# A chunked scan between dense matmuls: transposes first, a shared PSUM ring, two products on another engine

## The chip, the cores and the metric

The kernel runs on one core of a Trainium2 chip. Five engines work side by side, each with its own queue: TensorE (PE; its weight loads are listed as PEld), VectorE (DVE), ScalarE (ACT), GpSimd (POOL) and SyncE (SP), which here only issues DMAs. The metric is the device time of one execution in microseconds, median of several runs. [...]

## The reference, cut to what matters

One layer on 1024 tokens of width 1024: three token mixers (two attentions and a state space model), merged with sigmoid gates, and a gated MLP. The change lies in the state space model's scan. With x as 16 heads of 64, B and C as 2 groups of 128, dt per token and head, and a the running sum of dt*A in a chunk:

```python
xdt = xf * dtc[..., None]
decay = jnp.where(causal, jnp.exp(jnp.where(causal, seg, 0.0)), 0.0)   # seg = a_i - a_j
cb = jnp.einsum('bcign,bcjgn->bcijg', Cc, Bc)
y_diag = jnp.einsum('bcijg,bcijgh,bcjghp->bcighp', cb, decay, xdt)
states = jnp.einsum('bcjgn,bcjgh,bcjghp->bcghpn', Bc, decay_to_end, xdt)
def step(h, inp):
    st, dec = inp
    return h * dec[..., None, None] + st, h
y_off = jnp.einsum('bcign,bcghpn,bcigh->bcighp', Cc, h_in, jnp.exp(a_cum))
...
y = (y + xh * D[:, None]).reshape(Bsz, S, SSM_INNER)
return rms_norm(y * jax.nn.silu(z), norm_g)
```

## The kernel before

The program is a chain of stages; PE's order inside the stages around the change is written out by hand, while a scheduler sets the order of the other engines' queues from its own model of time. Two kinds of work are merged on PE:

- **The dense work** ("fill"): 36 column blocks of the input projection, that is 1728 matmuls of 128x512 (`mm`, L794; six of them per step of the generator, counted as 1.3 us). A block's weights are loaded (`wr`), split into a high part by ACT (`wh`, L744) and a low part by DVE (`wl`, L745); ACT evicts each half block (L801), and SP stores it to `g_d` (L808). The dense work depends on nothing in attention or scan, so it is put between their pieces, first in attention, then in the scan.
- **The scan** over eight chunks of 128 tokens. In step c of its loop, `ssd_a` prepares chunk c, `ssd_b` computes chunk c-1, `ssd_c` finishes chunk c-2, and `merge` interleaves them with a budget of dense work, `FILL_SSD[c]` in us of the generator's counting; what is not used is carried over. What is left of the dense work after the scan runs before the next stage.

`ssd_a`: `pcb` is C·B of a group of 8 heads (DVE masks it into `cbm`); `pse` are the exponents of four heads, which ACT turns into `E`; DVE multiplies E by cbm, and ACT and DVE split E into `Eh` and `El`. PE transposes the chunk of x (`xs`, loaded by L1062) into `stp`, and ACT copies this to `xT`, in two halves of 8 heads (g = 0, 1). From xT come three products of 128x1024: `xd` = x·dt (DVE, then split into `xdt` by ACT and DVE), `xdd` = x·decay_to_end·dt (GpSimd, L1113) and the start of `y` = x·D (GpSimd, L1115). `bT` is the transpose of B.

`ssd_b`: `py` are the products of E with xdt, which DVE adds to y; `pof` (L1136) is C times the incoming state, which DVE scales into `yo` and adds to y; `pst` (L1146) is B^T·xdd, which DVE adds to the state `hst` (L1152) after it has scaled the old one (L1151). Then y is multiplied by the gate z (L1155, DVE), squared and summed by ACT into `yss` (L1158, with the buffer `yT` as the place of the squares), and scaled by ACT with the inverse root that DVE finds (L1160, L148 to L159).

`ssd_c`: PE transposes y in two halves (L1171), ACT copies them to `yT` (L1172), and SP stores `yT` to `ys_d` (L1174). There is one `yT` buffer and one `xdd` buffer.

PSUM in the scan: two banks for `pcb` and `pse` ("seg"), two for `py`, one for every transpose ("tp"), one for `pof` and `pst` ("st"), two for the dense work. The stage behind the scan multiplies the three mixers' outputs by their weights (`ybr`, L167); it first loads `ar` and splits it into `ah` (ACT) and `al` (DVE).

Of the kernel before, what the change touches and what calls it, by code (L numbers as in the profile page):

```python
# [11 lines left out]
F32 = mybir.dt.float32  # L12
F32R = mybir.dt.float32r
BF16 = mybir.dt.bfloat16
I32 = mybir.dt.int32
AF = mybir.ActivationFunctionType
# [5 lines left out]
P = 128  # L22
# [20 lines left out]
def block_kernel(ctx: ExitStack, tc: tile.TileContext, x, positions, norm_mix_g, w_in, b_gate,  # L43
# [91 lines left out]
    def uid(s):  # L135
        cnt[0] += 1
        return f"{s}_{cnt[0]}"
# [845 lines left out]
        return 0.88 * jp + 0.33 + 0.39  # L983

    FILL_ATT = 1.08
    FILL_SSD = [10.6] * 8 + [12.0, 30.0]
    with ExitStack() as pt__:
        atp = pt__.enter_context(TP("atp", 2))
        psp = pt__.enter_context(TP("psa", 1, space=PSUM))
# [39 lines left out]
    with ExitStack() as ps__:  # L1029
# [37 lines left out]
        def ssd_a(o, c):  # L1067

            if c + 1 < NT:
                seg_rows(c + 1)  # L1070
                load_bc(obj[c + 1], c + 1)
            xT = pool.tile([P, D], F32, name=uid("xT"), tag="xT", bufs=1)
            o.E = []
            for g in range(2):
                hs = slice(8 * g, 8 * g + 8)
                pcb = psp.tile([P, 512], F32, name=uid("pcb"), tag="seg", bufs=2)
                T.matmul(pcb[:, 0:P], o.bc[:, g, :], o.bc[:, 2 + g, :], start=True, stop=True)
                cbm = pool.tile([P, P], F32, name=uid("cbm"), tag="cbm")
                V.tensor_mul(cbm, pcb[:, 0:P], tri)
                yield 0.22  # L1080
                for q in range(2):
                    pse = psp.tile([P, 512], F32, name=uid("pse"), tag="seg", bufs=2)
                    T.matmul(pse, seg_l[c % 2][:, 2 * g + q, :], seg_r[2 * g + q].rearrange("r h i -> r (h i)"),
                             start=True, stop=False)
                    T.matmul(pse, identb, mssd.rearrange("p h i -> p (h i)"), start=False, stop=True)
                    if c + 1 < NT:
                        seg_cols(c + 1, 2 * g + q)
                    E = pool.tile([P, 4, P], F32, name=uid("E"), tag="E")
                    A.activation(E, pse.rearrange("p (h i) -> p h i", h=4), AF.Exp)
                    V.tensor_mul(E, E, cbm.unsqueeze(1).to_broadcast([P, 4, P]))  # L1090
                    Eh, El = (pool.tile([P, 4, P], F32R, name=uid(n), tag=n, bufs=4) for n in ("Eh", "El"))
                    split(Eh, El, E)
                    o.E.append((Eh, El))
                    yield 0.43
                pt = psp.tile([P, 512], F32, name=uid("stp"), tag="tp", bufs=1)
                for j in range(4):
                    T.transpose(pt[:, j * P:j * P + P], o.xs[:, 4 * g + j, :], ident)
                A.activation(xT[:, 512 * g:512 * g + 512], pt, AF.Copy)
                yield 0.44
            if c + 1 < NT:  # L1100
                load_xs(obj[c + 1], c + 1)
            o.bT = pool.tile([P, 2, P], F32, name=uid("bT"), tag="bT")
            pt = psp.tile([P, 256], F32, name=uid("stp"), tag="tp", bufs=1)
            for g in range(2):
                T.transpose(pt[:, g * P:g * P + P], o.bc[:, g, :], ident)
            A.activation(o.bT, pt.rearrange("p (g n) -> p g n", g=2), AF.Copy)
            xv = xT.rearrange("p (h d) -> p h d", d=64)
            o.xdt = pool.tile([P, 16, P], F32R, name=uid("xdt"), tag="xdt")
            xd = pool.tile([P, 16, 64], F32, name=uid("xd"), tag="xd", bufs=1)
            V.tensor_mul(xd, xv, hb(dt, c))  # L1110
            split(o.xdt[:, :, 0:64], o.xdt[:, :, 64:128], xd)
            o.xdd = pool.tile([P, 16, 64], F32, name=uid("xdd"), tag="xdd", bufs=1)
            G.tensor_mul(o.xdd, xv, hb(dend, c))  # L1113
            o.y = pool.tile([P, 16, 64], F32, name=uid("y"), tag="y", bufs=3)
            G.tensor_mul(o.y, xv, Db.unsqueeze(2).to_broadcast([P, 16, 64]))  # L1115
            yield 0.22

        def ssd_b(o, c, prev):

            zt, _ = f_t4.get()  # L1120
            SY.dma_start(zt, z_d[c * P:c * P + P, :])
            for g in range(2):
                hs = slice(8 * g, 8 * g + 8)
                for q in range(2):
                    py = psp.tile([P, 4, P], F32, name=uid("py"), tag="py", bufs=2)
                    for hh in range(4):
                        h, (Eh, El) = 8 * g + 4 * q + hh, o.E[2 * g + q]
                        T.matmul(py[:, hh, :], Eh[:, hh, :], o.xdt[:, h, :], start=True, stop=False)
                        T.matmul(py[:, hh, 0:64], El[:, hh, :], o.xdt[:, h, 0:64], start=False, stop=True)
                    h4 = slice(8 * g + 4 * q, 8 * g + 4 * q + 4)  # L1130
                    V.tensor_add(o.y[:, h4, :], o.y[:, h4, :], py[:, :, 0:64])
                    V.tensor_add(o.y[:, h4, :], o.y[:, h4, :], py[:, :, 64:128])
                    yield 0.8
                if prev is not None:
                    po = psp.tile([P, 512], F32, name=uid("pof"), tag="st")
                    T.matmul(po, o.bc[:, 2 + g, :], prev.hst[:, hs, :], start=True, stop=True)  # L1136
                    tmp = pool.tile([P, 8, 64], F32, name=uid("yo"), tag="yo", bufs=1)
                    V.tensor_mul(tmp, po.rearrange("p (h d) -> p h d", d=64), hb(ea, c, hs))
                    V.tensor_add(o.y[:, hs, :], o.y[:, hs, :], tmp)
                    yield 0.86  # L1140
            if c + 1 < NT:
                o.hst = pool.tile([P, 16, 64], F32, name=uid("hst"), tag="hst")
                for g in range(2):
                    hs = slice(8 * g, 8 * g + 8)
                    ps_ = psp.tile([P, 512], F32, name=uid("pst"), tag="st")
                    T.matmul(ps_, o.bT[:, g, :], o.xdd[:, hs, :], start=True, stop=True)  # L1146
                    psv = ps_.rearrange("p (h d) -> p h d", d=64)
                    if prev is None:
                        V.tensor_copy(o.hst[:, hs, :], psv)
                    else:  # L1150
                        V.tensor_mul(o.hst[:, hs, :], prev.hst[:, hs, :], hb(cdec, c, hs))  # L1151
                        V.tensor_add(o.hst[:, hs, :], o.hst[:, hs, :], psv)  # L1152
                    yield 0.86
            yf = o.y.rearrange("p h d -> p (h d)")
            V.scalar_tensor_tensor(out=yf, in0=yf, scalar=0.5, in1=zt, op0=ALU.mult, op1=ALU.mult)  # L1155
            o.yT = pool.tile([P, 8, P], F32, name=uid("yT"), tag="yT", bufs=1)
            ss = pool.tile([P, 1], F32, name=uid("yss"), tag="yss")
            A.activation(o.yT.rearrange("p j s -> p (j s)"), yf, AF.Square, accum_out=ss)  # L1158
            v = pool.tile([P, 1], F32, name=uid("yv1"), tag="yv1")
            V.tensor_scalar(v, ss, 1.0 / D, EPS, op0=ALU.mult, op1=ALU.add)  # L1160
            r = pool.tile([P, 1], F32, name=uid("yr1"), tag="yr1")
            rsqrt(pool, r, v, 1)
            A.activation(yf, yf, AF.Copy, scale=r)

        def ssd_c(o, c):

            yf = o.y.rearrange("p h d -> p (h d)")
            for g in range(2):
                pt = psp.tile([P, 512], F32, name=uid("stp"), tag="tp", bufs=1)
                for j in range(4):  # L1170
                    T.transpose(pt[:, j * P:j * P + P], yf[:, (4 * g + j) * P:(4 * g + j + 1) * P], ident)  # L1171
                A.activation(o.yT[:, 4 * g:4 * g + 4, :], pt.rearrange("p (j s) -> p j s", j=4), AF.Copy)  # L1172
                yield 0.44
            SY.dma_start(ys_d[:, :, c * P:c * P + P].rearrange("j p s -> p j s"), o.yT)  # L1174

        with tc.manual_schedule(engines={mybir.EngineType.PE}):
# [3 lines left out]
            for q in range(4):  # L1180
                seg_cols(0, q)
            load_xs(obj[0], 0)
            merge([], 6.0)
            for c in range(NT + 2):
                st = []
                if c < NT:
                    st.append((ssd_a(obj[c], c), 3.4))
                if 0 <= c - 2 < NT:
                    st.append((ssd_c(obj[c - 2], c - 2), 0.88, 0.6 if c <= NT else 0.9))
                if 0 <= c - 1 < NT:  # L1190
                    st.append((ssd_b(obj[c - 1], c - 1, obj.get(c - 2)), 6.6, 0.25 if c < NT else 0.1))
                merge(st, FILL_SSD[c])
# [488 lines left out]
```

## Time and profile before

| | us |
|---|---|
| runs, median of 3 | 2163.03 (2156.59 to 2163.8) |
| profiled execution, time | 2163.26 |
| its span, first to last instruction | 2161.5 |
| TensorE clock granted, mean | 0.982 |

The profile is of one execution. Engine shares are shares of the span. A row of a windows table gives the length of a window, then busy time and number of instructions of PE, PEld, DVE, ACT and POOL, the granted clock of PE (1.00 is full), the DMA engines' share and GB/s. A row of waits reads: who waited, for whom, microseconds in total, times, longest. A row of the timeline gives start, duration, engine, line, operation, output<-inputs, and in brackets how long the engine stood idle before it and what ended that. The scan's first matmul starts at 989.2 us, its last at 1223.2.

### The profile page before, as it was taken

How to read it: one execution, taken by the hardware profiler on the slowest of the kernel's cores; microseconds unless marked ns; L12 is line 12 of the kernel's file. 1: busy time of each engine (PE TensorE's matmuls, PEld its weight loads, DVE VectorE, ACT ScalarE, POOL GpSimd, SP SyncE). 2: the span in 40 equal slices, each digit the busy share in tenths (PEclk: the TensorE clock that was granted, in tenths of full speed). 3: DMA queues.
4: the chain of work that ended last, by engine and by line, in shares of the span. 5: the costliest groups of instructions: out<-in, count | busy, mean ns of one | idle time of the engine just before them, and what ended most of it. 6: DMA issues, size and time to landing. Idle time of an engine off the chain costs nothing.

```text
span 2161.5 us, 29107 instructions
## 1 busy us (share of the span) xinstructions
PE 2053.6 (95%) x10239; PEld 1693.8 (78%) x10253; DVE 1406.9 (65%) x2574; ACT 933.7 (43%) x1669; POOL 689.9 (32%) x636
## 2 busy tenths in 40 slices
PE   7999899999999999999999999999889999999999
PEld 6898787778888787787666788888668888887887
DVE  6687477356656566665888446557976777665655
ACT  5554222145555555554445313223444444544432
POOL 2454132212222222220222022002655454441855
PEclk9999999999999999999999999999899999999999
DMA  5167668554343544524343556342122222229765
GB/s 168 33 186 223 228 211 247 196 147 126 100 131 108 125 125 107 128 87 119 92 117 94 169 178 209 116 151 79 39 88 88 78 88 78 87 71 346 250 210 194
DMA packets 276649, 303.61 MB, mean 140 GB/s; under 512 B 19308, under 2 KB 209784, under 8 KB 276504
## 3 DMA queue, kind: packets, MB, share of 16 engines
q1 hardware_dynamic: 276504, 301.76, 45.5%
q8 instruction: 81, 1.33, 0.3%
q14 instruction: 64, 0.52, 0.1%
HBM read 209.03 MB, written 92.67 MB: 140 GB/s over the span
## 4 chain that ended last, share of the span: by engine, by line
PE 76%; DVE 10%; DMA 5%; ACT 3%; issue 3%; POOL 2%; SPq 0%; DVEq 0%; ACTq 0%; POOLq 0%
PE mm L794 15%; PE dn L1628 10%; PE ybr L167 8%; PE ua L1321 5%; PE uc L1321 4%; PE ud L1321 4%; PE wo L1366 4%; PE fx L167 4%; PE s L884 4%; PE tp L952 3%; PE ub L1321 2%; PE cq L167 1%; PE fxv L167 1%; PE q L167 1%; PE kv L167 1%
## 5 line engine op out<-in xcount | busy, mean ns | idle before, releaser
L794 PE MATMUL mm<-hnh,wh 128*128 128x512 f32 x576 | 251.5, 437 | 0.0
L906 POOL TENSOR_SCALAR pm<-pm,rs 128x128 f32<-128x128 f32 (+7 forms) x128 | 109.6, 859 | 407.3 <-DVE rs L905 256.2
L794 PE MATMUL mm<-hnh,wl 128*128 128x512 f32 x576 | 228.1, 396 | 0.0
L794 PE MATMUL mm<-hnl,wh 128*128 128x512 f32 x576 | 227.3, 395 | 0.0
L1628 PE MATMUL dn<-dr,dr 128*128 128x512 f32 x592 | 182.2, 389 | 0.0
L899 ACT ACTIVATE pm<-s,nmx 128x128 f32<-128x128 f32 (+2 forms) x192 | 110.0, 578 | 98.7 <-DVE nmx L896 69.8
L958 DVE TENSOR_TENSOR ptl<-tp,pth 128x512 fp32r<-128x512 f32 (+1 forms) x160 | 100.3, 633 | 69.7 <-ACT pth L957 68.0
L889 DVE TENSOR_REDUCE nmx<-s 128x1 f32<-128x128 f32 (+2 forms) x192 | 105.6, 553 | 58.8 <-PE s L887 47.0
L884 PE MATMUL s<-qk,qk 96*128 96x384 f32 (+5 forms) x480 | 122.3, 359 | 12.7 <-ACT pm L899 11.0
L957 ACT ACTIVATE pth<-tp 128x512 fp32r<-128x512 f32 (+1 forms) x160 | 88.0, 553 | 100.7 <-PE tp L952 100.2
L1628 PEld LDWEIGHTS dn<-dr,dr 128*128 128x128 f32 x592 | 111.1, 188 | 23.1
L794 PEld LDWEIGHTS mm<-hnh,wl 128*128 128x128 f32 x576 | 109.1, 189 | 25.6
L794 PEld LDWEIGHTS mm<-hnl,wh 128*128 128x128 f32 x576 | 110.2, 191 | 17.8 <-issue 3.4
L794 PEld LDWEIGHTS mm<-hnh,wh 128*128 128x128 f32 x576 | 110.7, 192 | 17.1 <-issue 3.3
L1628 PE MATMUL dn<-dr 128*128 128x512 f32 x296 | 115.2, 389 | 0.0
L167 PE MATMUL fx<-w5h,hnh 128*128 128x512 f32 x256 | 101.9, 403 | 7.0 <-ACT w5h L142 7.0
L143 DVE TENSOR_TENSOR dr<-dr,dr 128x1024 fp32r<-128x1024 f32 x52 | 73.0, 1403 | 54.3 <-ACT dr L142 52.4
L142 ACT ACTIVATE wh<-wr 128x1024 fp32r<-128x1024 f32 (+1 forms) x46 | 41.9, 911 | 144.5 <-PE ybr L167 63.5
L884 PEld LDWEIGHTS s<-qk,qk 96*128 96x128 f32 (+1 forms) x480 | 82.2, 194 | 25.6 <-ACT pm L899 15.0
L167 PE MATMUL fx<-w5h,hnl 128*128 128x512 f32 x256 | 101.8, 399 | 0.0
L167 PE MATMUL ybr<-ah,wh 128*128 128x512 f32 x256 | 99.6, 394 | 1.6 <-ACT ah L142 1.6
L167 PE MATMUL fx<-w5l,hnh 128*128 128x512 f32 x256 | 101.1, 396 | 0.0
(457 smaller groups left out, 5819.1 us busy)
## 6 DMA issues: line engine op xcount, KB each, us to landing
dr<-act_d SPq DMA_DIRECT2D x99, 256.0 KB
wr<-in_ffn_w_up_dram SPq DMA_DIRECT2D x47, 512.0 KB
wr<-in_w_in_dram SPq DMA_DIRECT2D x36, 512.0 KB
g_d<-t SPq DMA_DIRECT2D x24, 512.0 KB
gl<-g_d SPq DMA_DIRECT2D x24, 512.0 KB
ws<-in_ffn_w_down_dram SPq DMA_DIRECT2D x22, 512.0 KB
wsum_d<-ws SPq DMA_DIRECT2D x22, 512.0 KB
act_d<-fa SPq DMA_DIRECT2D x22, 512.0 KB
```

Source lines behind the costliest of these rows:

```text
L143: return i, le.tensor_sub(l, src, f32(h))
L167: T.matmul(ps, a(k), b(k), start=(i == 0), stop=(i == n - 1))
L794: T.matmul(ps, a[:, k, :], b[half][:, k, :], start=(k == 0 and i == 0), stop=(k == NK - 1 and i == 2))
L884: T.matmul(ps[:, :w], q_[:, qs], k_[:, a:a + w], start=i_ == 0, stop=not last and i_ == len(o.passes) - 1)
L889: later(c + 0.1, lambda ps=ps, ci=ci, a=a, b=b: V.reduce_max(nmx[:, ci:ci + 1], ps[:, :b - a], axis=AX, negate=True))
L899: pss[ci][1][0] = later(c + 0.9 + 0.1 * ci, lambda ci=ci, a=a, b=b: A.activation(p_[:, a:b], pss[ci][0][:, :b - a], AF.Exp, bias=nb, accum ...
L906: G.tensor_scalar(p_[:, 0:n * P], p_[:, 0:n * P], rs[:, 3:4], 0.0, op0=ALU.mult, op1=ALU.add)
L957: later(c + 0.05, lambda th=th, pt=pt, off=off: A.activation(th[:, :off], pt[:, :off], AF.Copy))
L958: pl[0] = later(c + 0.6, lambda th=th, tl=tl, pt=pt, off=off: V.tensor_sub(tl[:, :off], pt[:, :off], f32(th[:, :off])))
L1321: T.matmul(ps, a, b, start=first and n == 0, stop=n == 11, skip_group_check=not first)
L1366: T.matmul(p, a, b, start=k == 0 and i == 0, stop=k == NK - 1 and i == 2)
L1628: T.matmul(ps[m], a[:, ts_], b[:, 512:], start=first_ and j == 0 and q == 0, stop=j == NFH - 1 and q == 2, skip_group_check=not first_)
```

## The change

`ssd_a` starts with the transposes of x and all that follows from xT, and loads the next chunk's x right behind them; then come the exponents. B's transposes are done one by one into the bank of `pcb`, behind C·B, and copied out by ACT in two parts. `xdd` and the first `y` are computed by VectorE. The transposes of x and y and the products `pof` and `pst` share one ring of two banks ("ts"). The dense budget is 12.0 us in chunks 0 to 8 (10.6, and 12.0 in the ninth, before) and 8.0 in the last step (30.0), and 10.0 ahead of the loop (6.0).

```diff
-    FILL_SSD = [10.6] * 8 + [12.0, 30.0]
+    FILL_SSD = [12.0] * 8 + [12.0, 8.0]
...
             xT = pool.tile([P, D], F32, name=uid("xT"), tag="xT", bufs=1)
+            for g in range(2):
+                pt = psp.tile([P, 512], F32, name=uid("stp"), tag="ts", bufs=2)
+                for j in range(4):
+                    T.transpose(pt[:, j * P:j * P + P], o.xs[:, 4 * g + j, :], ident)
+                A.activation(xT[:, 512 * g:512 * g + 512], pt, AF.Copy)
+                yield 0.44
+            if c + 1 < NT:
+                load_xs(obj[c + 1], c + 1)
...
+            V.tensor_mul(xd, xv, hb(dt, c))
+            split(o.xdt[:, :, 0:64], o.xdt[:, :, 64:128], xd)
+            o.xdd = pool.tile([P, 16, 64], F32, name=uid("xdd"), tag="xdd", bufs=1)
+            V.tensor_mul(o.xdd, xv, hb(dend, c))
+            o.y = pool.tile([P, 16, 64], F32, name=uid("y"), tag="y", bufs=3)
+            V.tensor_mul(o.y, xv, Db.unsqueeze(2).to_broadcast([P, 16, 64]))
...
                 cbm = pool.tile([P, P], F32, name=uid("cbm"), tag="cbm")
+                T.transpose(pcb[:, P:2 * P], o.bc[:, g, :], ident)
                 V.tensor_mul(cbm, pcb[:, 0:P], tri)
-                yield 0.22
+                A.activation(o.bT[:, g, :], pcb[:, P:2 * P], AF.Copy)
+                yield 0.33
...
-                pt = psp.tile([P, 512], F32, name=uid("stp"), tag="tp", bufs=1)
...
-            for g in range(2):
-                T.transpose(pt[:, g * P:g * P + P], o.bc[:, g, :], ident)
-            A.activation(o.bT, pt.rearrange("p (g n) -> p g n", g=2), AF.Copy)
...
-            G.tensor_mul(o.xdd, xv, hb(dend, c))
-            G.tensor_mul(o.y, xv, Db.unsqueeze(2).to_broadcast([P, 16, 64]))
...
-                    po = psp.tile([P, 512], F32, name=uid("pof"), tag="st")
+                    po = psp.tile([P, 512], F32, name=uid("pof"), tag="ts", bufs=2)
...
-                    ps_ = psp.tile([P, 512], F32, name=uid("pst"), tag="st")
+                    ps_ = psp.tile([P, 512], F32, name=uid("pst"), tag="ts", bufs=2)
...
-                pt = psp.tile([P, 512], F32, name=uid("stp"), tag="tp", bufs=1)
+                pt = psp.tile([P, 512], F32, name=uid("stp"), tag="ts", bufs=2)
...
-            merge([], 6.0)
+            merge([], 10.0)
...
-                    st.append((ssd_a(obj[c], c), 3.4))
+                    st.append((ssd_a(obj[c], c), 3.26))
```

What that does to the queues is seen at three places. First PE around the state products of chunk 3 (step 4 of the loop; `ident` marks a transpose, and `t_...` as its source is a chunk of x, `bc_...` is B). Before, with a dense group of six left out:

```order
L1097 MATMUL stp_12346<-ident,t_3962_12124 128x128 x4
L1171 MATMUL stp_12352<-ident,y_11887 128x128 x4
L1146 MATMUL pst_12359<-xdd_12136,bT_12126 128x512
...
L1105 MATMUL stp_12372<-ident,bc_11924 128x128 x2
L1146 MATMUL pst_12386<-xdd_12136,bT_12126 128x512
L1077 MATMUL pcb_12418<-bc_12170 128x128
```

The change, where the left-out rows are dense matmuls (two groups of six between the transposes) and the second matmul of pse:

```order
L1169 MATMUL stp_12417<-ident,y_11777 128x128 x4
L1144 MATMUL pst_12424<-xdd_12027,bT_12031 128x512
...
L1103 MATMUL pse_12434<-segr_11251,segl_11252 128x512
...
L1144 MATMUL pst_12446<-xdd_12027,bT_12031 128x512
L1076 MATMUL stp_12478<-ident,t_3993_12271 128x128 x4
...
L1076 MATMUL stp_12497<-ident,t_3993_12271 128x128 x4
```

The second group of chunk 4's x transposes stood ahead of the state products and B's between them; now the first two rows of transposes behind the second state product are chunk 5's, and B's have left the place.

Second, DVE at the same place, from the product with z on. Before:

```order
L1155 SCALAR_TENSOR_TENSOR y_12138<-y_12138,t_3992_12218 128x1024
L1110 TENSOR_TENSOR xd_12377<-xT_12172,dt 128x1024
L1152 TENSOR_TENSOR hst_12358<-hst_12358,pst_12359 128x512
L1151 TENSOR_TENSOR hst_12603<-hst_12358,cdec 128x512
L143 TENSOR_TENSOR xdt_12376<-xd_12377,xdt_12376 128x16x64
L1152 TENSOR_TENSOR hst_12358<-hst_12358,pst_12386 128x512
```

The change:

```order
L1153 SCALAR_TENSOR_TENSOR y_12029<-y_12029,t_3991_12258 128x1024
L143 TENSOR_TENSOR El_12408<-E_12404,Eh_12407 128x512
L1150 TENSOR_TENSOR hst_12423<-hst_12423,pst_12424 128x512
L1149 TENSOR_TENSOR hst_12675<-hst_12423,cdec 128x512
L1110 TENSOR_TENSOR E_12438<-E_12438,cbm_12390 128x512
L1087 TENSOR_TENSOR xdd_12278<-xT_12225,dend 128x1024
L1150 TENSOR_TENSOR hst_12423<-hst_12423,pst_12446 128x512
```

Chunk 4's xd stood ahead of the first state addition and is now done long before; its xdd, which GpSimd had, stands ahead of the second, and parts of E between.

Third, PE at the end of the scan: chunk 7's y (`y_13108`, in the change `y_13041`) and the next stage's first products. Before, with 72 dense matmuls from mm_13288 to mm_13342:

```order
L1171 MATMUL stp_13281<-ident,y_12873 128x128 x4
L794 MATMUL mm_13288<-hnh_129,wh_12996 128x512
...
L794 MATMUL mm_13342<-hnh_129,wl_13197 128x512
L1171 MATMUL stp_13368<-ident,y_13108 128x128 x4
L1171 MATMUL stp_13375<-ident,y_13108 128x128 x4
L167 MATMUL ybr_13449<-ah_13419,wh_13443 128x512
```

The change:

```order
L794 MATMUL mm_13280<-hnh_129,wl_12998 128x512
L1169 MATMUL stp_13361<-ident,y_12796 128x128 x4
L1169 MATMUL stp_13369<-ident,y_13041 128x128 x4
L1169 MATMUL stp_13376<-ident,y_13041 128x128 x4
L167 MATMUL ybr_13449<-ah_13419,wh_13443 128x512
```

The dense work ends ahead of chunk 6's last transposes, and chunk 7's follow directly. PE has 519 dense matmuls between the last attention product and the last transposes of y in both kernels; 9 of them stood ahead of the first `pcb` before, 45 do now, and in a steady chunk there are 54 instead of 48.

More of the change, by code (lines that the diff above doesn't have):

```diff
@@ L1072, in ssd_a @@
             xT = pool.tile([P, D], F32, name=uid("xT"), tag="xT", bufs=1)
+            for g in range(2):
[6 more added lines that the diff above has]
+                load_xs(obj[c + 1], c + 1)
+            xv = xT.rearrange("p (h d) -> p h d", d=64)
+            o.xdt = pool.tile([P, 16, P], F32R, name=uid("xdt"), tag="xdt")
+            xd = pool.tile([P, 16, 64], F32, name=uid("xd"), tag="xd", bufs=1)
+            V.tensor_mul(xd, xv, hb(dt, c))
[4 more added lines that the diff above has]
+            V.tensor_mul(o.y, xv, Db.unsqueeze(2).to_broadcast([P, 16, 64]))
             o.E = []
+            o.bT = pool.tile([P, 2, P], F32, name=uid("bT"), tag="bT")
             for g in range(2):
@@ L1094, in ssd_a @@
                     yield 0.43
-                pt = psp.tile([P, 512], F32, name=uid("stp"), tag="tp", bufs=1)
[L1096 to L1103, printed above, removed]
-            for g in range(2):
-                T.transpose(pt[:, g * P:g * P + P], o.bc[:, g, :], ident)
-            A.activation(o.bT, pt.rearrange("p (g n) -> p g n", g=2), AF.Copy)
[L1107 to L1116, printed above, removed]
         def ssd_b(o, c, prev):
```

## The prediction

> **What bounds the kernel now.** I read the page first, then the scan in windows, then the waits of TensorE (PE), then the timeline of one chunk and of the scan's end.
>
> ```profile
> span 2161.5 us, 29107 instructions
> ...
> PE 2053.6 (95%) x10239; PEld 1693.8 (78%) x10253; DVE 1406.9 (65%) x2574; ACT 933.7 (43%) x1669; POOL 689.9 (32%) x636
> ...
> PE 76%; DVE 10%; DMA 5%; ACT 3%; issue 3%; POOL 2%; SPq 0%; DVEq 0%; ACTq 0%; POOLq 0%
> ```
>
> PE is the bound of the whole program, so a gain can only be PE time that is idle or at a low clock. The change adds and removes no matmul of any size: what it can win is the idle time of PE between 984 and 1226 us, where the scan lies. Next, two steady chunks (the first and last of four), with their mean:
>
> ```profile
> 1079.54:1105.64 26.10, 23.93 (x118) 17.19 (x118) 22.09 (x41) 12.58 (x21) 5.14 (x3) 1.00 0.38 112
> ...
> 1157.65:1183.67 26.02, 23.84 (x117) 17.33 (x118) 21.59 (x40) 12.70 (x21) 5.15 (x3) 1.00 0.22 71
> sum 104.13, PE 95.42 PEld 69.22 DVE 88.22 ACT 50.46 POOL 20.60; mean PE 23.86 PEld 17.30 DVE 22.06 ACT 12.62 POOL 5.15
> ```
>
> A chunk takes 26.0 us; PE (first column after the length) works 23.86 of it and VectorE (DVE, third) 22.06. So 2.2 us a chunk are idle. The waits of PE, in 984 to 1000, 1000 to 1200 and 1200 to 1260:
>
> ```profile
> PE pcb L1077 <- DMA bc<-xbc_d: 3.2, 1, 3.2
> ...
> PE pst L1146 <- DVE hst L1152: 10.2, 6, 3.2
> PE stp L1171 <- ACT xT L1098: 3.4, 5, 0.7
> ...
> PE ybr L167 <- ACT ah L142: 1.6, 1, 1.6
> PE stp L1171 <- ACT yT L1172: 1.1, 1, 1.1
> ```
>
> Five waits, 19.5 us. Three are PSUM banks that the change doubles: the one bank of state products (pst waits until hst has read it) and the one of transposes (stp waits for the copy out of it, xT or yT). One is the scan's first load, one the first operand of the stage behind the scan. The longer ones also cost clock:
>
> ```profile
> 984.00:1000.00 16.00, 12.77 (x50) 8.83 (x49) 5.69 (x13) 3.95 (x7) 0.00 (x0) 0.89 0.45 129
> 1050.00:1066.00 16.00, 12.83 (x55) 8.77 (x54) 12.49 (x24) 6.94 (x11) 2.51 (x2) 0.89 0.34 100
> 1080.00:1096.00 16.00, 14.51 (x71) 10.56 (x69) 13.99 (x27) 8.45 (x13) 3.80 (x2) 1.00 0.34 100
> 1222.00:1236.00 14.00, 11.25 (x45) 8.72 (x44) 6.51 (x7) 6.16 (x9) 0.00 (x0) 0.88 0.85 265
> ```
>
> The granted clock (0.89) is 0.11 x 16 = 1.8 us short in the windows of the 3.2 us waits, and 0.12 x 14 = 1.7 us at the scan's end, but stays 1.00 where the wait was 1.5 us.
>
> **Part by part.** *Start.* 45 dense matmuls instead of 9 now stand on PE between the last attention product and pcb, and the transposes of xs, whose load is issued before the last attention stores, stand among them. 36 x 0.23 us = 8 us of cover is more than the 3.2 us wait: it goes, and with it the dip. **-3.2 and -1.8.**
>
> [...]
>
> *One ring of two banks.* In a chunk it serves in turn: xs transposes g0, g1, pof g0, y transposes g0, pof g1, y transposes g1, pst g0, pst g1 (g: half of the heads). The wait of pst g1 on hst g0 is gone, since pst g1 takes the other bank. The seam before:
>
> ```profile
> 1078.62 0.66 PE L1171 MATMUL stp<-ident,y 128*128 128x128 f32 x4 [0.69 <-ACT xT L1098]
> 1078.65 2.85 POOL L1115 TENSOR_TENSOR y<-xT,Db 128x1024 f32<-128x1024 f32 x1 [20.75 <-ACT xT L1098]
> 1079.12 1.02 PE L1146 MATMUL pst<-xdd,bT 128*128 128x512 f32 x2
> 1079.65 2.93 DVE L1110 TENSOR_TENSOR xd<-xT,dt 128x1024 f32<-128x1024 f32 x1
> 1082.50 0.68 DVE L1152 TENSOR_TENSOR hst<-hst,pst 128x512 f32<-128x512 f32 x1
> 1083.23 1.12 PE L1146 MATMUL pst<-xdd,bT 128*128 128x512 f32 x2 [1.49 <-DVE hst L1152]
> 1084.51 2.30 POOL L1113 TENSOR_TENSOR xdd<-xT,dend 128x1024 f32<-128x1024 f32 x1 [3.01 <-PE pst L1146]
> 1085.82 1.53 DVE L1151 TENSOR_TENSOR hst<-hst,cdec 128x512 f32<-128x512 f32 x1
> 1085.89 0.49 PE L1083 MATMUL pse<-segr,segl 10*128 10x512 f32 x1
> 1086.32 0.39 PE L1085 MATMUL pse<-mssd,identb 128*128 128x512 bf16 x1
> ...
> L1110 DVE TENSOR_TENSOR xd<-xT,dt x8: 1212/2926/2928, 1005.7 to 1182.7; 128x1024 f32<-128x1024 f32 x8
> L1151 DVE TENSOR_TENSOR hst<-hst,cdec 128x512 f32<-128x512 f32 x8 | 8.9, 1113 | 0.1
> ```
>
> pst g0 ends at 1080.1, but DVE reads it at 1082.5, behind an xd of 2.93 us. What is late next: (a) xs g0 of the next chunk needs hst g0. From the end of pof g1, PE has pse (0.8, rows 1085.89 and 1086.32), 6 dense (1.4 at 0.23 each, from the run of 72 below), y transposes (0.6), pst g0 (1.0), 6 dense, pse, pst g1: 7.0. DVE has yo, y, E and El (half-width like hst, 0.7 each), the z product (1.2) and hst, and waits 0.7 for ACT's exponential: done at about 5.4. (b) xs g1 needs hst g1, behind xdd, which itself waits for pst g1 (one xdd buffer): 7.0 + 0.7 (E still ahead of it) + 1.2 + 0.7 = 9.6, against PE at 7.0 + 0.6 (xs g0) + 2.8 (12 dense) = 10.4. 0.8 us to spare, the smallest margin that I find. (c) The weight split wl of a dense block comes on DVE behind two y additions in one chunk, about 0.5 us late. All pst waits go, with one dip: **-10.2 and -1.8**. The waits of y transposes on the xT copy go, since the xs transposes now stand a third of a chunk away: **-3.4**. New waits: bounds 0 and 1.49 us (the seam's old wait) in seven seams, 10.4; I take **+1.5**, near the lower end because of (a) and (b).
>
> *GpSimd's products on DVE.* xd takes 2.93 us beside GpSimd's y, 1.21 at its least; L1151 is 1.53 beside xdd and averages 1.11 with half of its instances alone, thus 0.69. GpSimd costs DVE 1.72 + 0.84 = 2.56 us a chunk; two products at 1.21 cost 2.42. DVE's 22.06 becomes 21.9. The cover is PE's chunk; were DVE to bound, this is worth 0.1 us.
>
> *Other moves, at nothing.* bT goes out of PSUM in two copies beside cbm, in pcb's bank; the next user but one of that bank is pse, with a dense group or products between. The xs load is issued after the first transposes and is used a chunk later; on SP behind it stand bc and ys_d with as much slack. Six more dense matmuls a chunk lengthen a chunk by 1.3 us and are taken from elsewhere: here the end.
>
> *End.* The dense work is the same in total, and the order shows that none is left behind the last products: 72 dense matmuls that stood between chunk 6's and chunk 7's y transposes are gone from there.
>
> ```profile
> 1204.70 0.60 PE L1171 MATMUL stp<-ident,y 128*128 128x128 f32 x4
> 1204.95 1.22 DVE L1155 SCALAR_TENSOR_TENSOR y<-y,t 128x1024 f32<-128x1024 f32 x1
> 1205.06 0.48 PE L794 MATMUL mm<-hnh,wh 128*128 128x512 f32 x1
> 1205.49 0.59 ACT L1172 ACTIVATE yT<-stp 128x512 f32<-128x512 f32 x1
> 1206.10 0.37 SPq L1174 DMA_DIRECT2D ys_d<-yT  x1
> ...
> 1209.40 1.06 ACT L1158 ACTIVATE yT<-y 128x1024 f32<-128x1024 f32 x1 [3.32 <-DMA ys_d<-yT]
> 1212.82 0.16 DVE L159 SCALAR_TENSOR_TENSOR yr<-rs_t,yr 128x1 f32<-128x1 f32 x1
> 1213.08 1.15 ACT L1163 ACTIVATE y<-y,yr 128x1024 f32<-128x1024 f32 x1 [1.27 <-DVE yr L159]
> ...
> 1221.51 0.60 PE L1171 MATMUL stp<-ident,y 128*128 128x128 f32 x4
> 1223.93 0.60 ACT L1172 ACTIVATE yT<-stp 128x512 f32<-128x512 f32 x1 [0.75 <-PE stp L1171]
> 1224.42 2.94 ACT L142 ACTIVATE ah<-ar 128x1024 fp32r<-128x1024 f32 x3
> 1225.52 1.22 PE L167 MATMUL ybr<-ah,wh 128*128 128x512 f32 x2 [1.63 <-ACT ah L142]
> ```
>
> Chunk 7's y is ready at 1214.2: its square goes into the one yT buffer, which must first be stored. Under 72 dense matmuls (1205.06 to 1221.51, 16.45 us) this was free. Now PE waits for it. Without the dense work before ends its tail at 1225.52 - 16.45 = 1209.1. After: 1214.2, plus the store's delay, since the last g_d store now stands just ahead of ys_d on SP (0 if they overlap, 3.3 us, ys_d's own time to land, if they follow each other; I take 1.5, about half); then stp 0.6, two yT copies 1.2, ah 1.0, and hand-overs 0.3: 3.1. ybr starts at 1218.8: **+9.7** (8.2 to 11.5). The clock dips there as before, **+0.3** for the longer idle time (0 to 1.7).
>
> **Sum:** -5.0 - 12.0 - 3.4 + 1.5 + 9.7 + 0.3 = -8.9 us. The profiled execution took 2163.26 us, 0.2 over the median of 2163.03, so 2154.4; I give 2154.5.
>
> **Rivals.** *A, the end takes all of it* (no measurable change): the gain of 20.4 stands, but the end costs 11.5 + 1.7 and every second seam waits 1.5 us: 2163.3 - 20.4 + 13.2 + 5.2 = 2161.3. For it: the whole tail chain is now exposed. Against it: ys_d's 3.3 us were mostly not transfer limits of anything else. 0.17.
> *B, the wait only moves* (no change): pst g0 now shares its bank with pof g1, so it waits for DVE's yo as pst g1 did for hst. At the old 10.2 us, with its dip, the sum is +3.1: 2166.4; at half, 2160.4. Against it: between pof g1 and pst g0 stand 3 us of PE work, before none for this bank. 0.13.
> *C, DVE blocks itself* (slower): xdd stands in DVE's queue and waits there for pst g1 on PE; before, GpSimd waited (3.01 us in the seam). Everything behind, hst g1 first, is held, and xs g1 on PE with it. It decides once hst g1 comes 0.8 + 8.9/7 = 2.1 us later than I reckon; slower by 6.5 us needs 0.8 + 15.4/7 = 3.0 us, and gives 2169.8. For it: 1082.50 above, where hst stood behind a long xd. Against it: without GpSimd no DVE operation is over 1.3 us. 0.10. [...]
> *D, better than forecast*: no new wait and the stores overlap: -20.4 + 8.2 = -12.2, 2151.1. 0.15.
>
> **How the numbers follow.** My forecast holds 0.45 (2152.5 to 2157.5), D 0.15, A 0.17, B 0.13, C 0.10. 0.3% is 6.5 us, about what a measurement of this kernel can tell from no change: faster is below 2156.5. That takes D and most of the forecast's share, 0.15 + 0.43; within 0.3%: the rest of it, A and B and a little of C, 0.33; slower 0.09. The range 2149 to 2163 leaves out C and half of B above, and below only a run like the lowest of before, 2156.59, which was 6.4 under the median.
>
> **What would show it.** Right: no PE wait of pcb on DMA at the start; a clock of 1.00 from 984 us on; chunks of 25.2 us (23.86 + 6 x 0.23) with PE idle under 0.3; no pst wait on hst; xd at 1.2 us and GpSimd idle; then one gap of 9 to 11 us on PE before chunk 7's y transposes, ended by ACT, and a clock dip behind it. Wrong: seams with PE waiting for hst g1 or yo, chunks over 26 us, or an end with less than 6 us of gap.

## The result, and the profile after

The changed kernel takes 2145.62 us (median of 4 runs, 2142.28 to 2148.36) against 2161.82 us for the kernel before in the same job: ratio 0.9926 [0.991, 0.9942]. It is faster by 0.7%, as forecast, but by more than forecast, and the time lies below the range given. The profiled execution took 2144.91 us. First the page of after, then the windows of the scan (from the last attention product to the first `ybr`) and of the stage behind it, before and after:

```profile
span 2143.0 us, 29100 instructions
...
PE 2042.3 (95%) x10253; PEld 1689.7 (79%) x10253; DVE 1402.9 (65%) x2590; ACT 936.0 (44%) x1677; POOL 649.0 (30%) x620
```

```profile
983.52:1225.52 242.00, 221.67 (x1061) 163.49 (x1074) 176.36 (x321) 109.40 (x172) 40.20 (x16) 0.99 0.36 111
1225.52:1401.40 175.88, 175.88 (x768) 145.30 (x769) 94.20 (x119) 46.95 (x60) 24.86 (x16) 0.99 0.56 178
```

```profile
978.55:1207.35 228.80, 216.70 (x1076) 162.76 (x1074) 171.53 (x337) 110.60 (x180) 0.00 (x0) 0.98 0.40 120
1207.35:1384.33 176.98, 176.98 (x769) 146.35 (x769) 94.04 (x119) 47.04 (x60) 24.88 (x16) 0.98 0.54 173
```

By the two profiles the scan is 13.2 us shorter and the stage behind it 1.1 longer: 12.1 us. The other 6.4 us of the two spans lie in stages whose code is the same. The waits of PE in 1200 to 1260 (in 984 to 1200 the view has no row at all), and windows that answer to those of the prediction: the start, two steady stretches, the end:

```profile
PE stp L1169 <- ACT y L1161: 10.4, 1, 10.4
PE ybr L167 <- ACT ah L142: 1.6, 1, 1.6
```

```profile
984.00:1000.00 16.00, 16.00 (x75) 12.04 (x74) 8.66 (x11) 7.18 (x13) 0.00 (x0) 1.00 0.76 213
1079.00:1104.00 25.00, 25.00 (x127) 18.63 (x126) 21.66 (x45) 12.99 (x22) 0.00 (x0) 1.00 0.45 130
1100.00:1125.00 25.00, 24.89 (x126) 18.54 (x124) 21.47 (x42) 12.74 (x22) 0.00 (x0) 1.00 0.46 138
1200.00:1214.00 14.00, 8.62 (x25) 6.87 (x26) 6.36 (x14) 6.67 (x9) 0.00 (x0) 0.52 0.55 170
```

In the steady chunks PE is idle for at most 0.11 us in a window, at full clock. What is left is one long gap at the end; in its window PE works 8.62 of 14 us, at a clock of 0.52. Two stretches of the timeline, the seam that the prediction reckoned through, and the end (only the rows of the chain):

```profile
1071.40 1.02 PE L1144 MATMUL pst<-xdd,bT 128*128 128x512 f32 x2
...
1072.81 0.68 DVE L1150 TENSOR_TENSOR hst<-hst,pst 128x512 f32<-128x512 f32 x1
...
1074.39 1.02 PE L1144 MATMUL pst<-xdd,bT 128*128 128x512 f32 x2
...
1075.25 0.60 PE L1076 MATMUL stp<-ident,t 128*128 128x128 f32 x4
...
1075.89 1.22 DVE L1087 TENSOR_TENSOR xdd<-xT,dend 128x1024 f32<-128x1024 f32 x1
...
1077.03 0.68 DVE L1150 TENSOR_TENSOR hst<-hst,pst 128x512 f32<-128x512 f32 x1
...
1078.46 0.60 PE L1076 MATMUL stp<-ident,t 128*128 128x128 f32 x4
...
1192.79 0.60 PE L1169 MATMUL stp<-ident,y 128*128 128x128 f32 x4
...
1193.04 1.23 DVE L1153 SCALAR_TENSOR_TENSOR y<-y,t 128x1024 f32<-128x1024 f32 x1
...
1194.47 0.37 SPq L1172 DMA_DIRECT2D ys_d<-yT  x1
...
1199.39 1.06 ACT L1156 ACTIVATE yT<-y 128x1024 f32<-128x1024 f32 x1 [4.94 <-DMA ys_d<-yT]
...
1202.54 1.15 ACT L1161 ACTIVATE y<-y,yr 128x1024 f32<-128x1024 f32 x1 [2.00 <-DVE yr L159]
...
1203.74 1.97 PE L1169 MATMUL stp<-ident,y 128*128 128x128 f32 x8 [10.36 <-ACT y L1161]
...
1207.35 1.22 PE L167 MATMUL ybr<-ah,wh 128*128 128x512 f32 x2 [1.63 <-ACT ah L142]
```

DVE's hst now starts 0.4 us after the end of the first state product, and neither transpose group waits for its bank. At the end, chunk 7's y is ready at 1194.3, its square starts at 1199.4, once yT has been stored, and PE stands idle for 10.4 us.

### The profile page after: what moved, and what is told of

It reads as the page before. It is cut to its first block, busy times and chain, and to the rows that moved or that the text cites. A ratio compares the mean times of both kernels' runs of the same rounds, so it can differ in the third digit from the quotient of the medians.

```text
span 2143.0 us, 29100 instructions
## 1 busy us (share of the span) xinstructions
PE 2042.3 (95%) x10253; PEld 1689.7 (79%) x10253; DVE 1402.9 (65%) x2590; ACT 936.0 (44%) x1677; POOL 649.0 (30%) x620
## 4 chain that ended last, share of the span: by engine, by line
PE 78%; DVE 7%; DMA 5%; POOL 3%; ACT 3%; issue 3%; SPq 0%; DVEq 0%; ACTq 0%; POOLq 0%
PE mm L794 16%; PE dn L1626 10%; PE ybr L167 8%; PE ua L1319 5%; PE fx L167 5%; PE uc L1319 5%; PE ud L1319 4%; PE wo L1364 4%; PE s L884 3%; PE tp L952 2%; PE ub L1319 2%; PE fxv L167 1%; DMA raw<-in_w_in_dram 1%; PE kv L167 1%; PE q L167 1%
## 5 line engine op out<-in xcount | busy, mean ns | idle before, releaser
L794 PEld LDWEIGHTS mm<-hnl,wh 128*128 128x128 f32 x576 | 109.2, 190 | 17.1 <-issue 2.9
L1235 POOL TENSOR_TENSOR mg<-mg,gl 128x512 f32<-128x512 f32 x16 | 24.9, 1561 | 311.4 <-DVE gl L1232 311.3
```

Source lines behind the costliest of these rows:

```text
L794: T.matmul(ps, a[:, k, :], b[half][:, k, :], start=(k == 0 and i == 0), stop=(k == NK - 1 and i == 2))
```

## Experiments

The kernel before ran beside all of them: 2157.76 us (19 runs, beside e1 to e4), 2160.56 (7 runs, e5 to e8), 2160.9 (11 runs, e9 to e12). "The scan" is the window from the last attention product to the first `ybr`.

**e1, the old budgets in the changed kernel.** 72 dense matmuls stand again ahead of chunk 7's transposes.

```diff
-    FILL_SSD = [12.0] * 8 + [12.0, 8.0]
+    FILL_SSD = [10.6] * 8 + [12.0, 30.0]
...
-            merge([], 10.0)
+            merge([], 6.0)
```

> The changed kernel with the dense budgets of before (6.0 ahead of the loop, 10.6 in eight chunks, 12.0 and 30.0 at the end): 72 dense matmuls stand again ahead of chunk 7's y transposes. Theory 'waits' (the gain is idle time of PE in the scan, of which the uncovered end gives back about 10 us of idle time and a longer spell at half clock): the stage from the last attention product to the first product behind the scan shrinks from 228.8 us to 217-218, the gap of 10.4 us is gone, 2134 us in all. Rival 'end is free' (what PE does not wait for there it waits for a little later, for loads): no change, 2144 to 2147 us.

2135.18 us, ratio 0.9908 [0.9883, 0.9932]. Its scan and its waits:

```profile
983.76:1206.42 222.66, 217.73 (x1061) 164.03 (x1074) 171.22 (x337) 110.06 (x180) 0.00 (x0) 0.98 0.40 120
```

```profile
PE ybr L167 <- ACT ah L142: 2.1, 1, 2.1
PE stp L1169 <- ACT y L1161: 1.5, 1, 1.5
```

The end's gap is gone and 6.1 us of the scan with it, so the time is where 'waits' put it; the scan missed the 217 to 218 expected, with a new wait of 1.5 us for the scaled y. The state products do not wait, nor does `pcb` at the start, with 27 dense matmuls ahead of it. So the new spread of dense work is a loss inside this change, and the removed waits did not need it.

**e2, the new budgets alone**, the same two lines edited the other way in the kernel before.

> The kernel before with the budgets of the change alone (10.0 ahead, 12.0 in nine chunks, 8.0 at the end). Theory 'waits': the start's wait and dip go (-5), the pst and stp waits stay, the end is uncovered (+10 idle, +1.5 clock): stage 242.0 to about 248.5, 2168 us. Rival 'cover' (six more dense matmuls a chunk, 1.4 us, are what hides the waits): the 1.49 us pst waits go too, -10 to -12: stage about 237, 2157 us.

2160.41 us, ratio 1.0018 [1.0007, 1.0029], scan 246.0 us instead of 242.0. The waits:

```profile
PE stp L1171 <- ACT y L1163: 10.4, 1, 10.4
PE pst L1146 <- DVE hst L1152: 8.3, 6, 2.9
PE stp L1171 <- ACT xT L1098: 2.9, 4, 0.8
```

The start's wait is covered, the end pays the same 10.4 us as in the change, and the state products keep most of theirs: six more dense matmuls a chunk hide 1.9 us of the old 10.2. The loss lies between what the two theories gave, nearer to 'waits'.

**e3, GpSimd's products back on GpSimd** in the changed kernel.

```diff
-            V.tensor_mul(o.xdd, xv, hb(dend, c))
+            G.tensor_mul(o.xdd, xv, hb(dend, c))
...
-            V.tensor_mul(o.y, xv, Db.unsqueeze(2).to_broadcast([P, 16, 64]))
+            G.tensor_mul(o.y, xv, Db.unsqueeze(2).to_broadcast([P, 16, 64]))
```

> The changed kernel with the two products back on GpSimd. Theory 'waits' with the ring as its cause: pst keeps its second bank, so DVE operations take up to 2.9 us again beside GpSimd's but PE waits little: 0 to +3 us, 2146 to 2149. Rival 'engine' (the products' move, which frees DVE of blocked operations, is what removed the waits): the pst waits come back, +10 to +13 us, 2156 to 2159.

2145.22 us, ratio 0.9943 [0.9924, 0.9961], scan 229.0 us against 228.8. In the new order the engine of the two products is worth nothing in time; what it does to the slack is seen at e4.

**e4, the old budgets with the 36 more dense matmuls ahead of the scan kept**: `FILL_SSD` of e1, `merge([], 10.0)` of the change.

> The changed kernel with 10.6 in the eight chunks and 30.0 at the end, and its 10.0 ahead of the loop: 48 dense matmuls (11.1 us) stand ahead of chunk 7's y transposes. Theory 'waits': they cover the 10.4 us gap; stage 217-218 us, 2134 us, and the half clock behind the scan shrinks from 17 us to 3-4. Rival 'end is free': 2144 to 2147.

2155.94 us, ratio 0.9994 [0.9977, 1.001]: a miss for both theories. The scan, the waits, and PE's clock at the longest of them:

```profile
979.94:1219.99 240.05, 222.36 (x1060) 166.48 (x1073) 171.43 (x337) 109.77 (x180) 0.00 (x0) 0.96 0.37 111
```

```profile
PE stp L1169 <- ACT y L1161: 13.4, 5, 4.1
```

```profile
1116.00:1126.00 10.00, 6.68 (x26) 5.55 (x27) 4.43 (x12) 2.65 (x4) 0.00 (x0) 0.66 0.00 0
```

A new wait in five chunks: y's transposes for the scaled y. The timeline of one of them, from one chunk's transposes to the next one's:

```profile
1097.52 0.60 PE L1169 MATMUL stp<-ident,y 128*128 128x128 f32 x4
...
1097.63 1.22 DVE L1153 SCALAR_TENSOR_TENSOR y<-y,t 128x1024 f32<-128x1024 f32 x1
...
1098.28 0.58 ACT L1170 ACTIVATE yT<-stp 128x512 f32<-128x512 f32 x1
...
1099.29 0.58 SPq L1172 DMA_DIRECT2D ys_d<-yT  x1
...
1106.41 1.06 ACT L1156 ACTIVATE yT<-y 128x1024 f32<-128x1024 f32 x1 [1.75 <-DMA ys_d<-yT]
...
1111.42 0.15 DVE L159 SCALAR_TENSOR_TENSOR yr<-rs_t,yr 128x1 f32<-128x1 f32 x1
...
1115.48 0.15 DVE L159 SCALAR_TENSOR_TENSOR yr<-rs_t,yr 128x1 f32<-128x1 f32 x1
...
1117.87 0.15 DVE L159 SCALAR_TENSOR_TENSOR yr<-rs_t,yr 128x1 f32<-128x1 f32 x1
...
1118.11 1.15 ACT L1161 ACTIVATE y<-y,yr 128x1024 f32<-128x1024 f32 x1 [0.43 <-DVE yr L159]
...
1119.32 0.90 PE L1169 MATMUL stp<-ident,y 128*128 128x128 f32 x3 [4.09 <-ACT y L1161]
```

This is a loop over the one yT buffer: transposes, copy, store, square into yT, root, scale, next transposes. y has its product with z at 1098.9, but the square stands until the store has landed, 7.1 us after its issue. The root's steps are 0.15 us long and come 2.4 to 4.1 us apart, between other DVE work. From these transposes to the next chunk's first it takes 21.8 us, and the two transpose groups of one chunk take the rest. In the changed kernel the loop has nothing to spare: its rows at the same place, one chunk earlier, are

```profile
1063.65 1.15 ACT L1161 ACTIVATE y<-y,yr 128x1024 f32<-128x1024 f32 x1 [0.23 <-DVE yr L159]
...
1064.86 0.66 PE L1169 MATMUL stp<-ident,y 128*128 128x128 f32 x4
```

The scale ends at 1064.80 and PE's transposes start at 1064.86. The same 0.06 us lie between the two in e4 (1119.26 and 1119.32), where PE did wait: it is the hand-over, not slack. In three of six steady seams of the changed kernel the scale ends within 0.2 us of the transposes, and at one of them PE is held for the 0.11 us of the window above. In e3, with the two products on GpSimd, the scale is done 3.8 to 4.7 us ahead in four of these seams: the products on VectorE cost no time, but they go with the loss of that slack. Six dense matmuls a chunk less, and e4 is over the edge. Whether e4's budgets would fit with the products on GpSimd was not run. e1 has the same number of dense matmuls a chunk as e4 and waits once, so that number alone does not decide; that the rest is the place of the root's steps in DVE's queue, as the scheduler set it, is likely and not shown.

**e5, e4 with the square out of the loop.** The square is written for its sum alone, so it can go to a tile that is dead, that of z.

```diff
-            A.activation(o.yT.rearrange("p j s -> p (j s)"), yf, AF.Square, accum_out=ss)
+            A.activation(zt, yf, AF.Square, accum_out=ss)
```

> The kernel is e4_dense_end, with one line changed: the squares of y go into the z tile, which is dead by then, and not into yT. Theory 'chain': y's transposes in e4 waited 13.4 us because of a loop over yT: transposes of y, copy into yT, store of yT (3 to 5 us), square into yT, root in steps on DVE between other work, scale, transposes of the next y. Without the store in it the scale comes 3 to 5 us sooner, so of the waits (2.85, 1.64, 4.09, 3.14, 1.67) at most 1 us is left, the half-clock spells behind them go, and the scan is 222 to 226 us instead of 240.1: 2134 to 2140 us. Rival 'DVE': DVE is what is late, the steps of the root stand behind E and y work that follows PE, and an earlier square does not move them: waits of 8 us or more stay, and the time stays at 2151 to 2158.

2137.3 us, ratio 0.9908 [0.9875, 0.9941]:

```profile
975.31:1196.56 221.25, 215.76 (x1060) 162.22 (x1073) 170.39 (x337) 109.44 (x180) 0.00 (x0) 0.99 0.40 120
```

```profile
PE stp L1169 <- ACT y L1161: 1.0, 1, 1.0
```

One line takes 12.4 of the 13.4 us of these waits and, with their low clock (0.96 over the scan of e4, 0.99 here), 18.8 us of the scan. 'Chain' held.

**e6, the same line in the changed kernel.**

> The changed kernel with the squares of y in the z tile. Theory 'chain': at the end the square of chunk 7 need not wait for the store of chunk 6's yT: it starts right behind the product with z (1194.4 instead of 1199.4), so the gap ahead of chunk 7's y transposes falls from 10.4 to 5.5 us and the time from 2145.6 to 2140 (2138 to 2142). Rival: another thing ends last there (the scale behind other ACT work, or ah's load, which waits for a buffer of the z tiles): gap of 8 us or more, or a new wait of ybr that takes the gain: 2144 to 2147.

2141.51 us, ratio 0.9921 [0.9892, 0.9949], scan 223.4 us, 5.4 less than in the change:

```profile
1194.38 1.23 DVE L1153 SCALAR_TENSOR_TENSOR y<-y,t 128x1024 f32<-128x1024 f32 x1
...
1195.67 1.06 ACT L1156 ACTIVATE t<-y 128x1024 f32<-128x1024 f32 x1
...
1200.02 1.97 PE L1169 MATMUL stp<-ident,y 128*128 128x128 f32 x8 [5.30 <-ACT y L1161]
```

The square follows the product with z at once, and the gap is 5.3 us instead of 10.4. So half of the end's gap was the wait for the store.

**e7, the ring alone in the kernel before; e8, the ring, and B's transposes in the bank of pcb.** Neither moves x's transposes. Of e7's diff, the lines for pof, pst and the transposes of x and y (the last two read alike; B's move into the ring in the same way):

```diff
-                pt = psp.tile([P, 512], F32, name=uid("stp"), tag="tp", bufs=1)
+                pt = psp.tile([P, 512], F32, name=uid("stp"), tag="ts", bufs=2)
...
-                    po = psp.tile([P, 512], F32, name=uid("pof"), tag="st")
+                    po = psp.tile([P, 512], F32, name=uid("pof"), tag="ts", bufs=2)
...
-                    ps_ = psp.tile([P, 512], F32, name=uid("pst"), tag="st")
+                    ps_ = psp.tile([P, 512], F32, name=uid("pst"), tag="ts", bufs=2)
```

> The kernel before with only the ring of two banks (old order, B's transposes in the ring, products on GpSimd, old budgets). B's transposes stand between the two state products, so the second has the bank of the first again. Theory 'order': the pst waits on hst stay (8 to 11 us in sum, with the dip), the stp waits on xT go: 2154 to 2159, scan 236 to 240. Rival 'banks': more banks alone take the waits: under 3 us of pst waits, scan about 230, 2146 to 2150.

> e7 with B's transposes in the bank of pcb. Now a transpose group of x stands between the two state products in the old order, so the second again shares the bank of the first, but DVE's hst stands ahead of xd in its queue. Theory 'order': what counts is how soon DVE gets to hst, so the pst waits shrink to 0 to 4 us without any x transposes moved: scan 229 to 235, 2146 to 2152. Rival: only x transposes at the front of the chunk end the waits: pst waits 6 us or more, scan above 236.

One run each: 2163.17 and 2151.51 us, both inside what the kernel before took beside them (2151.11 to 2165.34), so the scans decide: 243.7 and 240.4. The waits of e7, then of e8:

```profile
PE pst L1146 <- DVE hst L1152: 8.3, 5, 1.8
PE pst L1146 <- ACT bT L1106: 2.8, 1, 2.8
```

```profile
PE py L1126 <- DVE xdt L143: 8.1, 3, 6.2
PE pse L1086 <- ACT bT L1082: 5.4, 6, 1.1
```

e7's mechanism is 'order' as expected: with two banks the waits for hst stay at 8.3 of 10.2 us while the second state product falls on the bank of the first. Waits for bT came on top (2.8 us), and its scan and time are above what either theory gave. In e8 the state products no longer wait, as 'order' had it, but the price came back as waits that it did not name: py for xdt (6.2 of the 8.1 us in one chunk; in the old order xdt starts late in the chunk), and pse for the bank from which bT is copied. Its scan of 240.4 missed the 229 to 235 and lies where the rival had it, above 236, though not for the rival's reason.

**e9, the changed kernel without the ring**: the tags of x's and y's transposes, of pof and of pst edited back, so transposes have one bank, pof and pst the other.

> The changed kernel without its ring: every transpose again in the one bank it had before, pof and pst in the other one (the same two banks, split as before); order, bT's place, engines and budgets are those of the change. Theory 'order': in the trace of the change hst g0 ends 0.9 us ahead of the second state product (1073.49 against 1074.39) and each copy out of a transpose bank at least 0.5 us ahead of the next transposes, so no wait needs the ring: no PE wait over 0.3 us before the last y transposes, scan 229, 2142 to 2149. Rival 'ring': the second bank is what takes the waits: pst or stp waits of 5 us or more in sum come back, scan over 234, 2151 or more.

2144.3 us, ratio 0.9935 [0.9914, 0.9955], scan 231.0 us. Its longest wait ahead of those at the end (10.3 us for the scaled y, 1.6 for ah):

```profile
PE stp L1076 <- ACT xT L1077: 1.0, 2, 0.8
```

No state product waits: the ring is not what took those waits away. It is worth 2.2 us of the scan, where 'order' had none, and nothing that the time shows (e10, the ring's kernel in the same job, took 2145.35). The order does the rest, that is the places of x's and of B's transposes together. In the new order the two were not parted.

**e10, the changed kernel once more, in 6 runs.**

> The changed kernel itself once more, beside the kernel before. By the traces the region of the change (scan and the stage behind) is 12.1 us shorter, and the rest of 18.5 us came from stages with the same code. Theory 'rest is chance': over more runs the difference is 11 to 14 us (ratio 0.9935 to 0.995). Rival 'rest belongs to the change': 16 us or more (ratio 0.9925 or lower).

2145.35 us, ratio 0.9938 [0.9921, 0.9955], that is 13.4 us [9.7, 17.1] of 2160.9. The scan is 228.8 us and the stage behind it 176.8, as in the first profile. By the profile the gain of the change is 12.1 us. The ratio lies in the range of 'rest is chance', but the difference of the two medians is 15.6, and the interval reaches the 16 us of the rival. So 'rest is chance' is the likelier, and the rival is not excluded.

**e11, e1 with the square in the z tile.**

> e1_old_budget with the squares of y in the z tile: the end is covered and the loop over yT is shorter. Its one wait of 1.5 us for the scale and its dip go: scan 220 to 222 (222.7 in e1), 2132 to 2137. Rival: e5's shift of waits, in which the scheduler places DVE's work otherwise and new waits of 1 us or more come up elsewhere: scan 222 to 225, 2135 to 2140.

2135.02 us, ratio 0.9886 [0.9867, 0.9904]: the lowest ratio here, though its interval overlaps that of e1, and 10.3 us under the changed kernel in the same job. Its scan, the shortest of all and 2.5 us below what was expected, and its only wait:

```profile
976.89:1194.38 217.49, 215.38 (x1076) 161.72 (x1074) 171.56 (x337) 109.56 (x180) 0.00 (x0) 1.00 0.41 122
```

```profile
PE ybr L167 <- ACT ah L142: 2.1, 1, 2.1
```

**e12, the two products alone on VectorE in the kernel before.** e3's edit the other way round.

> The kernel before with only GpSimd's two products on VectorE. DVE has y's product behind xd in its queue, both ahead of hst: 2.4 us where xd beside GpSimd took 2.93, so hst comes 0.5 us sooner. Theory 'order': the pst waits stay at 6 to 9 us, scan 239 to 242, GpSimd idle. Rival 'GpSimd': its load on DVE was the cause of the waits: pst waits under 3 us, scan under 235.

One run, 2153.84 us, scan 236.0 us:

```profile
PE pst L1146 <- DVE hst L1152: 6.8, 6, 2.6
```

The state products keep 6.8 of 10.2 us of waits, as 'order' had it. The scan is shorter than it gave, by 6.0 instead of 0 to 3: 3.4 us are these waits, and by the windows of the two scans PE is busy for 219.82 us instead of 221.67, 1.85 less, about what one dip takes in the prediction's windows (1.8). That this second part is not the move's doing is the author's estimate. So by this one profile the engine move is worth some 3.4 us in the old order, where hst stands behind xd, and nothing (e3) in the new one. The two do not add.

## Why the prediction was right in direction and short in size

**What held.** The waits named as removed are gone: start, state products, xT copies. Full clock from 984 us (1.00, below it again only from 1196.3); 25.2 us a chunk (the second y transposes start at 1071.0 and, four chunks on, at 1171.7); GpSimd idle; xd 1.2 us. The margins of the seam were reckoned at 1.6 us for (a) and 0.8 for (b); the rows above give 1.8 (hst ends at 1073.49, transposes start at 1075.25) and 0.75 (1077.71 and 1078.46). The end, +9.7 forecast, is 10.2: from chunk 6's last transposes to `ybr` 14.56 us, against 20.82 with 16.45 of dense work. Rival A fell: the end did not take all. Rivals B and C fell: no wait for yo, none behind xdd. The part of D on new waits came true, not its part on overlapping stores; that its sum of -12.2 is nearly the -12.1 of the profiles is luck, since its end was 2.0 us too cheap and its gain 3.0 too small.

**What failed: the cause given for the largest term.** The prediction had the waits for hst go "since pst g1 takes the other bank", and named the banks, beside the new place of x's transposes, for the copies too ("PSUM banks that the change doubles"). e9 has no second bank and no wait for hst; e7 has the two banks in the old order and keeps 8.3 us. What removed the waits is that hst no longer stands behind xd in DVE's queue and that B's and x's transposes have left the place between and ahead of the state products. The start is alike: its term rested on 36 more dense matmuls as cover, and in e1, with 18 of them, the wait is gone as well. The waits would be gone by either cause, so the measured time does not show this error; the runs do.

**What failed: the base.** "The profiled execution took 2163.26 us, 0.2 over the median of 2163.03, so 2154.4" took three runs and one profile for the kernel. The stages with unchanged code, span less scan and the stage behind, took 1743.6 us in that profile. In the 14 profiles of this study they take 1732.5 to 1743.6, mean 1737.9, and the two profiles of the changed kernel have 1737.2 and 1733.7. By them the base was 5.7 us high, from an execution at the top of the spread, and 5.7 of the 8.9 us between forecast and time are that. This is an account by profiles and not a measured split: the median of the kernel before came out 1.2 us under 2163.03 beside the result and 2.1 to 5.3 us under it in the later jobs. What makes the other stages vary was not followed up.

**What failed: the terms.** By the two profiles the sum of -8.9 measures -12.1, which is the other 3.2:

- *"New waits: ... I take +1.5"*: the view of waits has none. (a) and (b) said so; the 1.5 was a hedge that no margin asked for.
- *"-10.2 and -1.8", "-3.4"*: the gain from start, seams and xT is 23.4 us (the scan's 13.2 and the end's 10.2), not 20.4. A wait in this view counts from the modelled end of the matmul before. From start to start, the 12 state products behind a transpose took 12.46 us before, and 0.109 each where nothing waits (0.656 for six after): 11.15 instead of 10.2. The five transposes that waited for xT cost 4.25 in the same way, instead of 3.4, and behind each wait for hst the state product's second matmul followed 0.53 to 0.71 us after its first instead of 0.43, 0.8 in sum. These are 2.6 of the 3.0.
- *End and clock*: +0.5 and +0.8. The low clock behind the gap of 10.4 us lasts until 1213.3, 6.0 us into the stage behind, which is 1.1 us longer where 0.3 was forecast.

**The range.** Its lower end, 2149, allowed "only a run like the lowest of before", so it held neither a base that is high as a whole nor a gain larger than the waits view lists. The largest chance, 0.58 for faster, was on what came.

**Missed altogether: where the margin was smallest.** The prediction called 0.8 us "the smallest margin that I find". The loop over yT, which it worked through for the end alone, runs in every chunk, and in the changed kernel nothing is left of its slack in two seams. It cost 0.1 us here; e4 shows what it costs once it does not fit, 13.4 us of waits and their low clock (0.96 over the scan).

## What to carry to other kernels

When a wait for a PSUM bank goes by turning the order, look for the loop that is now the tightest: follow each single buffer around (copy, store, next writer) and compare its length with the chunk. A result that is written only for its sum belongs in a dead tile, where there is one, rather than in a buffer with a store in flight. Before a forecast is anchored, ask how far stages with unchanged code vary; a few us of spread there outweigh the terms of the sum.

## What the runs showed of the hardware

The low clock does not follow the length of a wait alone. In the kernel before, the wait of 3.23 us at the start went with a clock of 0.50 from 989.6 to 993.0, while the window 1080 to 1096, with the wait of 1.49 us, has 1.00. The scan of e1 has two waits of over 0.2 us, 1.5 ahead of y's transposes and 2.1 at its end, and a clock of 0.98; that of e11 has the one of 2.1 alone, and 1.00. In e4 the window 1116 to 1126, at the end of the wait of 4.09 us, has 0.66, and that of 1090 to 1100, in which PE is idle for 1.42 us, has 1.00.

In the profiles of the kernel before and of the change the clock inside the program is at 0.50 for 3.4, 6.8, 10.3, 13.7 or 17.1 us at a time, one to five times the shortest. The gap of 10.4 us in the change went with 17.1 us of it, from 1196.3 to 1213.3. The stage behind the scan has a clock of 0.98 behind the gap of 10.4 us in e10, and of 0.99 behind that of 10.3 in e9. What sets the length of these spells, and when one starts, is not shown.
